# An encoder block on one NeuronCore: w_down of three groups by Strassen's seven products, alternating with the next group's w_up

## The chip, the cores and the metric

The kernel runs on one core of a Trainium2 chip. The metric is the device time in microseconds of one execution, taken as the median of the runs; lower is better. A core has five engines that run side by side, each with its own in-order instruction stream: PE (TensorE, matrix products into PSUM), DVE (VectorE) and POOL (GpSimd) for elementwise work, ACT (ScalarE) for activations and copies, and SP (SyncE), which here issues all the DMAs.

## The reference, cut to what matters

One layer over 512 tokens and 1024 channels: an RMSNorm, a wide input projection, three token mixers (a state-space layer, a pooling mixer, banded attention), a gated merge, and then the MLP that the change is in:

```
h  = h + merged @ w_out                       # 512 x 1024
hn = rmsnorm(h, norm_mlp)
h  = h + square(relu(hn @ w_up)) @ w_down     # w_up 1024 x 4096, w_down 4096 x 1024
out = rmsnorm(h, norm_final)
```

All data is float32.

## The kernel before, in words

**Three products for one.** Every float32 matrix is split into a high part (rounded to the matmul's input format, fp32r) and a low part (what is left). A product is then high x high + high x low + low x high: `mm3` (L119) issues three matmuls. ACT makes the high part by a copy and DVE the low part by a subtraction.

**Weights.** All weight pieces stand in one list, `pieces`, in the order of their use; a piece has 128 partitions x 1024 elements (512 KB). `raw_to` (L172) lets SP load piece after piece into three `raw` buffers; `split_ops` (L182) gives the two instructions that split one into `wh` and `wl`, which have two buffers each. `use(i)` (L223) is called when the product with piece i begins, and schedules the split of piece i+1.

**What sets the order.** The program is written out by hand. A counter, `tick()` (L136), advances by one after each group of three matmuls, and `later(n, f)` (L132) puts `f` into the streams of its engines n ticks on. A tick is thus a place in the program, not a wait: an engine runs ahead of PE as far as its operands and buffers allow.

**The MLP.** The 4096 hidden columns are worked in four groups of 1024 (L1311). For each group, eight *units* of w_up: one 128-column piece of w_up stands still, and the 512 tokens of `hT` move past it, so eight `mm3` over the 1024 input channels fill one PSUM tile (24 matmuls of 128x512). `relu2` (L1302) takes it out: relu on ACT (L1306), the square on DVE (L1307), the high copy on ACT, the low part on DVE. Then `tokmajor` (L394) multiplies the group with w_down, first for the output columns 0 to 511, then for 512 to 1023: four PSUM tiles of 128 tokens x 512 columns, and for each of eight 128-row slices of w_down (two in a piece) and each of the four token tiles one `mm3`. That is 96 matmuls for a half and 192 for a group. `add_all` (L1250) adds the four tiles to the residual `h_t` on DVE. In the last group the second half is done token tile by token tile (`tok_inner`, L1259), so that the final norm of a tile overlaps the next one's product; for that the pieces of its second half are of kind "z" and keep their split tiles.

**Memory.** The elementwise tiles come from one pool `z` of 38 tiles of 128x512.

Of the kernel before, what the change touches and what calls it, by code (L numbers as in the profile page):

```python
# [9 lines left out]
F32 = mybir.dt.float32  # L10
# [45 lines left out]
def trunk(ctx: ExitStack, tc: tile.TileContext, a: dict, out):  # L56
# [4 lines left out]
    def pool(name, bufs=1, **kw):  # L61
        return ctx.enter_context(tc.tile_pool(name=name, bufs=bufs, reuse_waits="tile", **kw))
# [7 lines left out]
    xT_p = pool("xT")  # L70
    raw_p = pool("raw", NRAW)
    w_p = pool("w", 2)
    z_p = pool("z", NZ)
    ps_p = pool("ps", 8, space=PSUM)

    def z(dt=F32, n=512):
# [85 lines left out]


    pieces = []
    state = {"raw": 0, "split": 0}
    raws, splits = {}, {}

    def add_piece(src, kind="w"):
        pieces.append((src, kind))
        return len(pieces) - 1  # L170

    def raw_to(i):  # L172
        while state["raw"] <= min(i, len(pieces) - 1):
            k = state["raw"]
# [5 lines left out]
            state["raw"] += 1  # L180

    def split_ops():  # L182

        i = state["split"]
        state["split"] += 1
        src, kind = pieces[i]
        A, B = src.shape[1], src.shape[2]
        box = {}
        he = VE if i == 0 else SE

        def high():
# [12 lines left out]
        def low():
            r = box["r"]
            if kind == "z":
                for k in range(A):
                    tt(box["l"][k], r[:, k], fr(box["h"][k]), SUB)
            else:
                l = w_p.tile([128, 1024], F32R, tag="wl", name="wl")[:, 0:A * B].rearrange("p (a b) -> p a b", a=A)  # L210
# [3 lines left out]
            raw_to(i + NRAW)  # L214

        return high, low

# [47 lines left out]
    P_up, P_dn = [], []  # L265
    for g in range(4):
        P_up.append([add_piece(cols(w_up, 1024 * g + 128 * m)) for m in range(8)])
        P_dn.append([[], []])
        for x in range(8):
            i, hf = (x // 2, x % 2) if g == 3 else (x % 4, x // 4)  # L270
            P_dn[g][hf].append(add_piece(rows(w_down, 8 * g + 2 * i, 2, 512 * hf), "wz"[hf] if g == 3 else "w"))
# [6 lines left out]
    kz = [[const.tile([128, 512], F32R, name=f"kz{b}{r}") for r in range(2)] for b in range(2)]  # L278
    for b in range(2):
        for r in range(2):  # L280
            GE.memset(fr(kz[b][r][64 - 64 * b:128 - 64 * b]), 0.0)

    def gvec(name):
        g = gv_p.tile([128, D], F32, tag="g", name="g")
# [15 lines left out]
    right1 = tc.alloc_tile_pool(name="s5", bufs=1, side="right", reuse_waits="tile")  # L300
    prep_p = tc.alloc_tile_pool(name="prep", bufs=1, side="right", reuse_waits="tile")
    XS = right1.tile([128, 64, 2, 2, 16], F32, name="XS")
    Ud = tc.dram_tile([512, 512], F32, name="Ud")
    Fd = tc.dram_tile([2, 8, 4, 2, 512], F32, name="Fd")
    Kd = tc.dram_tile([512, 240], F32, name="Kd")
# [993 lines left out]
        norm_rows(t, g_mlp, hn_t[t])  # L1299
    g_fin = gvec("norm_final")  # L1300

    def relu2(p, aT_h, aT_l):  # L1302
        r, h, l = z(), zr(), zr()
        aT_h.append(h)
        aT_l.append(l)
        SE.activation(out=r, in_=p, func=AF.Relu)  # L1306
        later(1, lambda: tt(r, r, r, MUL))  # L1307
        later(2, lambda: copy(SE, h, r))
        later(3, lambda: tt(l, r, fr(h), SUB))

    for g in range(4):  # L1311
        aT_h, aT_l = [], []
        m0 = 0
        if g == 0:

            us = []
            for half in range(2):
                o = slice(256 * half, 256 * half + 256)
                for m in range(2):
                    if half == 0:  # L1320
                        us.append((splits[P_up[0][0]] if m == 0 else use(P_up[0][1]), ps()))
                    (hs, ls), p = us[m]
                    for k in range(8):
                        mm3(p[:, o], hs[k], ls[k], hT_h[k][:, o], hT_l[k][:, o], k == 0, k == 7)
                        if k % 2 == 1 and half == 1:
                            tick()
                if half == 0:
                    to_feature(hn_t[3], hh_, hl_, 3)
            for m in range(2):
                relu2(us[m][1], aT_h, aT_l)  # L1330
            m0 = 2
        for m in range(m0, 8):
            run(unit_quanta(P_up[g][m], hT_h, hT_l, lambda p: relu2(p, aT_h, aT_l)))
        add_all(0, tokmajor(P_dn[g][0], aT_h, aT_l))
        if g < 3:
            add_all(1, tokmajor(P_dn[g][1], aT_h, aT_l))
    for t in range(3):
        p = tok_inner(P_dn[3][1], aT_h, aT_l, t)
# [15 lines left out]
    for q in range(2):  # L1354
        p = ps()
        c, hc = slice(256 * q, 256 * q + 256), slice(512 + 256 * q, 768 + 256 * q)
        for k in range(8):
            hs, ls = splits[P_dn[3][1][k // 2]]
# [13 lines left out]
    ts(o[:, 512:768], hg[:, 512:768], rs, 1.0, MUL, MUL)  # L1372
    SP.dma_start(out=out[tok, 512:768], in_=o[:, 512:768])
    h_p.release()

# [67 lines left out]
```

## Time and profile before

| | us |
|---|---|
| median of 3 runs | 963.36 (959.46 to 963.53) |
| the profiled execution, its own time | 961.09 |
| its span from the first to the last instruction | 959.3 |
| PE busy in the span | 935.1 (97%) |
| DVE busy | 543.1 (57%) |
| ACT busy | 404.5 (42%) |
| POOL busy | 248.9 (26%) |

The engines overlap, so the busy times don't add up to the span. The profile's line on the ended chain follows the work backwards from the last instruction, at each step to what released it, and gives each engine its share of the span. A matmul row's length includes its way through the array, and successive matmuls overlap; how fast they follow one another is read from the distance of their starts. The first w_up unit of the MLP is taken out at 613.1 us of the span, and the MLP reaches to its end.

### The profile page before, as it was taken

What the parts mean: (1) busy time and instruction counts of PE and PEld (TensorE: products, weight loads), DVE (VectorE), ACT (ScalarE), POOL (GpSimd) and SP (SyncE); (2) the same over time, 40 slices, a digit from 0 to 9 for tenths busy, and PEclk for the clock granted to TensorE, in tenths of its full rate; (3) what the DMA queues carried; (4) which work ended last, traced back from release to release, by engine and by line L of the source; (5) the groups of instructions that cost most, each with busy time, mean ns of one, the idle gap of its engine ahead of it and who ended that gap; (6) DMA issues with size and microseconds to landing.
All of it is one profiled execution on the core that took longest, in us unless ns stands there. A gap on an engine that the chain in (4) does not pass through costs nothing.

```text
span 959.3 us, 12810 instructions
## 1 busy us (share of the span) xinstructions
PE 935.1 (97%) x4755; PEld 751.1 (78%) x4755; DVE 543.1 (57%) x892; ACT 404.5 (42%) x662; POOL 248.9 (26%) x402
## 2 busy tenths in 40 slices
PE   8999899999999999998999999999999999999997
PEld 5788667777677888886878888888888888888886
DVE  4688778886644765568555355443344345334443
ACT  5634656666654334455343333432133123313432
POOL 0600355556788885243100001000000000000002
PEclk9999989999999999999999999999999999999999
DMA  9237666642222334344512373223332332323322
GB/s 312 87 111 203 169 168 179 162 133 83 83 66 75 93 101 128 98 126 122 152 45 88 110 239 90 66 88 110 91 97 97 108 89 89 110 88 90 109 88 87
DMA packets 140462, 111.05 MB, mean 116 GB/s; under 512 B 16368, under 2 KB 117104, under 8 KB 140400
## 3 DMA queue, kind: packets, MB, share of 16 engines
q1 hardware_dynamic: 140400, 110.24, 38.9%
q8 instruction: 37, 0.61, 0.3%
q14 instruction: 25, 0.20, 0.1%
HBM read 106.32 MB, written 3.90 MB: 115 GB/s over the span
## 4 chain that ended last, share of the span: by engine, by line
PE 85%; DVE 6%; DMA 3%; issue 2%; ACT 1%; SPq 1%; POOL 1%; POOLq 0%; DVEq 0%; ACTq 0%
PE ps L122 25%; PE ps L123 25%; PE ps L121 25%; PE ps L781 3%; PE ps L765 2%; DVE z L103 2%; DVE z L106 1%; DVE wl L103 1%; PE ps L735 1%; PE ps L734 1%; DMA z<-in_s_bq_im_dram 1%; DVE S L738 1%; ACT z L96 1%; DMA z<-in_xT_dram 1%; SPq L1078 1%
## 5 line engine op out<-in xcount | busy, mean ns | idle before, releaser
L103 DVE TENSOR_TENSOR wl<-raw,wh 128x1024 fp32r<-128x1024 f32 (+1 forms) x137 | 172.8, 1261 | 157.7 <-ACT wh L96 157.2
L96 ACT ACTIVATE wh<-raw 128x1024 fp32r<-128x1024 f32 (+1 forms) x136 | 142.9, 1051 | 136.3 <-PE ps L123 99.8
L121 PE MATMUL ps<-xh,wh 128*128 128x512 f32 x384 | 156.5, 407 | 0.0
L103 DVE TENSOR_TENSOR z<-z 128x512 f32<-128x512 f32 (+1 forms) x132 | 102.2, 777 | 93.1 <-ACT z L1306 60.8
L123 PE MATMUL ps<-xh,wl 128*128 128x512 f32 x384 | 150.7, 392 | 2.9 <-DVE wl L103 2.9
L122 PE MATMUL ps<-xl,wh 128*128 128x512 f32 x384 | 150.2, 391 | 0.0
L122 PE MATMUL ps<-wl,z 128*128 128x512 f32 x320 | 125.5, 392 | 3.2 <-DVE wl L103 3.2
L121 PE MATMUL ps<-wh,z 128*128 128x512 f32 x320 | 125.6, 393 | 1.8 <-ACT z L318 0.9
L123 PE MATMUL ps<-wh,z 128*128 128x512 f32 x320 | 125.5, 392 | 0.2
L109 POOL TENSOR_SCALAR sm<-sm 128x1 f32<-128x1 f32 (+1 forms) x16 | 3.6, 223 | 459.6 <-ACT hn L1285 434.0
L122 PE MATMUL ps<-hl,wh 128*128 128x512 f32 (+1 forms) x272 | 102.5, 377 | 0.3 <-DVE hl L103 0.3
L121 PE MATMUL ps<-hh,wh 128*128 128x512 f32 (+1 forms) x272 | 102.5, 377 | 0.3 <-ACT hh L96 0.3
L123 PE MATMUL ps<-hh,wl 128*128 128x512 f32 (+1 forms) x272 | 102.4, 377 | 0.0
L96 ACT ACTIVATE z<-ps 128x512 f32<-128x512 f32 (+4 forms) x128 | 72.9, 578 | 64.5 <-PE ps L123 24.2
L123 PEld LDWEIGHTS ps<-xh,wl 128*128 128x128 f32 x384 | 72.3, 188 | 19.1 <-DVE wl L103 3.3
L121 PEld LDWEIGHTS ps<-xh,wh 128*128 128x128 f32 x384 | 72.7, 189 | 14.1 <-PE ps L781 0.8
L122 PEld LDWEIGHTS ps<-xl,wh 128*128 128x128 f32 x384 | 72.7, 189 | 12.9
L109 POOL TENSOR_SCALAR S<-S,sm 128x512 f32<-128x512 f32 x64 | 59.2, 942 | 81.2 <-DMA z<-Ud 58.6
L122 PEld LDWEIGHTS ps<-wl,z 128*128 128x128 f32 x320 | 60.5, 189 | 17.0 <-DVE wl L103 4.5
L121 PEld LDWEIGHTS ps<-wh,z 128*128 128x128 f32 x320 | 60.5, 189 | 15.6 <-ACT z L318 1.9
L123 PEld LDWEIGHTS ps<-wh,z 128*128 128x128 f32 x320 | 60.4, 189 | 13.4 <-DVE z L106 1.0
L745 ACT ACTIVATE S<-S,sm 128x512 f32<-128x512 f32 x64 | 46.2, 722 | 57.6 <-DVE sm L109 52.4
(183 smaller groups left out, 1437.9 us busy)
## 6 DMA issues: line engine op xcount, KB each, us to landing
raw<-in_w_in_dram SPq DMA_DIRECT2D x55, 512.0 KB
raw<-in_w_up_dram SPq DMA_DIRECT2D x32, 512.0 KB
raw<-in_w_down_dram SPq DMA_DIRECT2D x32, 512.0 KB
T<-in_ttab_dram SPq DMA_DIRECT2D x16, 448.0 KB
z<-Fd SPq DMA_DIRECT2D x16, 256.0 KB
raw<-in_w_branch_attn_dram SPq DMA_DIRECT2D x8, 512.0 KB
raw<-in_w_out_dram SPq DMA_DIRECT2D x8, 512.0 KB
z<-in_xT_dram SPq DMA_DIRECT2D x8, 256.0 KB
```

What stands on the lines that cost most here:

```text
L96: SE.activation(out=o, in_=i, func=AF.Copy, scale=scale)
L103: (eng or VE).tensor_tensor(out=o, in0=i, in1=j, op=op)
L106: VE.scalar_tensor_tensor(out=o, in0=i, scalar=s, in1=j, op0=op0, op1=op1)
L109: (eng or VE).tensor_scalar(out=o, in0=i, scalar1=s1, scalar2=s2, op0=op0, op1=op1)
L121: TE.matmul(o, wh, xh, start=first, stop=False)
L122: TE.matmul(o, wh, xl, start=False, stop=False)
L123: TE.matmul(o, wl, xh, start=False, stop=last)
L734: TE.matmul(p, lh, khh[h], start=True, stop=False)
L735: TE.matmul(p, lh, kll[h], start=False, stop=True)
L745: SE.activation(out=s, in_=s, func=AF.Exp, bias=nm, accum_out=den[h][:, t:t + 1])
L765: TE.transpose(p[:, t * 128:t * 128 + 128], probs[h][t][:, kt * 128:kt * 128 + 128], ident)
L781: TE.matmul(p[64 * b:64 * b + 64], vt[kt][h // 8][:, c:c + 64], pts.pop((h, kt)), start=kt == 0, stop=kt == 3)
```

## The change

In groups 0, 1 and 2 the 512 x 1024 by 1024 x 1024 product with w_down is cut into halves in all three directions, and the eight products of a 256-token half with a 512 x 512 block of w_down become the seven of Strassen's method (in Winograd's form, with shared sums). The blocks of the activation are A11, A12, A21, A22 (tokens by hidden columns), and those of w_down B11 to B22.

**Sums.** S1 to S4 are sums of activation blocks (S1 and S2 on DVE, S3 and S4 on POOL), T1 to T4 sums of w_down blocks (POOL, each in two pieces). T2, T3 and T4 are written over B11, B12 and B21. Each sum is an instruction over 128x1024 elements. Splitting into high and low parts comes after the sums: a piece of kind "s" is split from a block of w_down or from a T, and `a_split` splits a block of the activation.

**Products.** `product(g, x)` is 2 pieces x 2 slices x 2 token tiles x 3 matmuls of 128x512. The results of products that share terms stay in the same PSUM tiles: the chain "b" runs through products 2, 4 and 6, "c" through 3 and 5, and after each of these two tiles are added to `h_t`. Product 0 goes to two tiles `X` in SBUF, which POOL adds to `h_t` once, after the third group.

**Order.** Product x of group g is followed by unit x of group g+1, and unit 7 of group g+1 stands alone behind product 6. `plan(g)` gives the places of the sums, splits and loads. A product is 8 ticks and a unit is 8 ticks, so a group takes 120 ticks, and product x starts at tick 16x.

**Other parts.** `use` schedules two pieces ahead where a piece of kind "s" is near; `wh` and `wl` have a third buffer during the MLP. The square of the relu moves from DVE to ACT, written in place into a tile `R` of 128 x 4 x 512; high and low parts of the activation are made later, in groups 0 to 2 by `a_split` and in the last group by `a3`. w_down of groups 0 to 2 is loaded by `b_load` into tiles of its own, not into `raw`. The last group's product with w_down is done as before, by `tokmajor` and `tok_inner`.

The core of the diff:

```diff
     def use(i):
...
         d = SPLIT_AT
+        if "s" in [kind for _, kind in pieces[i:i + 3]]:
+            j, d = i + 2, 1
...
+    DN = ("11", "21", "T2", "T1", "T3", "22", "T4")
...
+    def relu2(p, g, m):
...
+        SE.activation(out=r, in_=p, func=AF.Relu)
+        later(1, lambda: SE.activation(out=r, in_=r, func=AF.Square))
...
+    AN = ("A11", "A12", "S2", "S1", "S3", "S4", "A22")
+
+    def a_split(g, x):
...
+    def b_load(g, nm):
+        k0, c0 = (0, 4)[nm[0] == "2"], (0, 512)[nm[1] == "2"]
+        for q in range(2):
+            t = Bt[g, nm, q] = str_p.tile([128, 2, 512], F32, tag=f"B{nm}{q}", name=f"B{nm}")
+            SP.dma_start(out=t, in_=rows(w_down, 8 * g + k0 + 2 * q, 2, c0))
+
+    def b_sum(g, nm, q, i, j, op):
+
+        at = {"T2": "11", "T3": "12", "T4": "21"}.get(nm)
+        o = Bt[g, at, q] if at else str_p.tile([128, 2, 512], F32, tag=f"{nm}{q}", name=nm)
+        tt(o, Bt[g, i, q], Bt[g, j, q], op, GE)
+        Bt[g, nm, q] = o
...
+    def plan(g):
...
+        at(4, *a_split(g, 1))
+        at(6, lambda: a_sum(g, "S1", lambda: ra[:, :, T1], lambda: rb[:, :, T1], ADD, VE))
+        at(8, lambda: a_sum(g, "S2", S("S1"), lambda: ra[:, :, T0], SUB, VE))
+        at(18, *a_split(g, 2))
+        at(22, lambda: a_sum(g, "S4", lambda: rb[:, :, T0], S("S2"), SUB, GE))
+        for n, x in ((34, 3), (50, 4), (66, 5), (82, 6)):
+            at(n, *a_split(g, x))
+        for q in range(2):
+            at(2 + 4 * q, lambda q=q: b_sum(g, "T3", q, "22", "12", SUB))
+            at(12 + 4 * q, lambda q=q: b_sum(g, "T2", q, "T3", "11", ADD))
+            at(36 + 4 * q, lambda q=q: b_sum(g, "T4", q, "21", "T2", SUB))
+        if g < 2:
+            for n, nm in ((44, "11"), (76, "12"), (92, "22"), (108, "21")):
+                at(n, lambda nm=nm: b_load(g + 1, nm))
+            at(112, lambda: b_t1(g + 1))
...
+    CH = (("a", None), ("d", (0, 0)), ("b", (0, 1)), ("c", (1, 1)), ("b", (1, 1)), ("c", (0, 1)), ("b", (1, 0)))
+
+    def product(g, x):
...
+                    TE.matmul(acc[t], ah[:, k, o], hs[i], start=st, stop=False, **kw)
+                    TE.matmul(acc[t], al[:, k, o], hs[i], start=False, stop=False, **kw)
+                    TE.matmul(acc[t], ah[:, k, o], ls[i], start=False, stop=sp, **kw)
+                    tick()
+        for t in range(2):
+            if to is None:
+                later(1 + t, lambda t=t: add_x1(g, t, acc[t]))
+            else:
+                later(1 + t, lambda t=t: add_to(2 * to[0] + t, to[1], acc[t]))
...
-    for g in range(4):
-        aT_h, aT_l = [], []
...
-        for m in range(m0, 8):
-            run(unit_quanta(P_up[g][m], hT_h, hT_l, lambda p: relu2(p, aT_h, aT_l)))
-        add_all(0, tokmajor(P_dn[g][0], aT_h, aT_l))
-        if g < 3:
-            add_all(1, tokmajor(P_dn[g][1], aT_h, aT_l))
...
+    def a3(m):
+        h, l = zr(), zr()
         aT_h.append(h)
         aT_l.append(l)
...
+        r = R[3, m // 4][:, m % 4]
+        copy(SE, h, r)
+        tt(l, r, fr(h), SUB)
...
+    for g in range(3):
+        plan(g)
+        for x in range(7):
+            product(g, x)
+            up_unit(g + 1, x)
+        if g == 2:
...
+            for m in range(4):
+                later(2 * m, lambda m=m: a3(m))
+        up_unit(g + 1, 7)
+    for m in range(4, 8):
+        later(2 * m - 7, lambda m=m: a3(m))
+    for n in range(8):
+        later(2 + 2 * n, lambda n=n: x1_out(n // 2, n % 2))
+    add_all(0, tokmajor(P_dn3[0], aT_h, aT_l))
```

On PE, before, the last three matmuls of group 0's last unit (`hh`, `hl` are the tokens, `wh`, `wl` the split weights) and the first three with w_down (`z` is the activation's high, then low part):

```order
L121 MATMUL ps<-hh,wh 128x512
L122 MATMUL ps<-hl,wh 128x512
L123 MATMUL ps<-hh,wl 128x512
L121 MATMUL ps<-wh,z 128x512
L122 MATMUL ps<-wl,z 128x512
L123 MATMUL ps<-wh,z 128x512
```

Behind these follow 189 more of the same form.

On PE, now, the end of group 0's first product (`ah`, `al` are the split block of the activation) and the beginning of group 1's first unit:

```order
L1443 MATMUL ps<-wh,ah 128x512
L1444 MATMUL ps<-wh,al 128x512
L1445 MATMUL ps<-wl,ah 128x512
L121 MATMUL ps<-hh,wh 128x512
L122 MATMUL ps<-hl,wh 128x512
L123 MATMUL ps<-hh,wl 128x512
```

Of the matmuls the form stays, and their order moved: runs of 192 with w_down and 192 with w_up become runs of 24 of either. PE's whole stream has 3835 rows before and 3763 now.

The second place is in the last group, where `tokmajor` begins behind the last w_up unit. On ACT, before: the high part of the first w_down piece, then the last unit's relu (L1306) and high part, a "z" piece, and the high part of the second w_down piece:

```order
L96 ACTIVATE wh<-raw 128x1024
L1306 ACTIVATE z<-ps 128x512
L96 ACTIVATE z<-z 128x512
L96 ACTIVATE z<-raw 128x512 x2
L96 ACTIVATE wh<-raw 128x1024
```

Between the relu and the second piece's `wh` stand three copies.

On ACT, now, at the same place, from the last unit's relu on (L1344 relu, L1345 square, `z<-R` the high parts of `a3`):

```order
L1344 ACTIVATE R<-ps 128x512
L1345 ACTIVATE R<-R 128x512
L96 ACTIVATE z<-R 128x512
L96 ACTIVATE z<-raw 128x512 x2
L96 ACTIVATE z<-R 128x512 x2
L96 ACTIVATE wh<-raw 128x1024
```

Between them stand now a square and five copies.

On DVE at the same place, before (the first piece's `wl`, the square and the low part of the last unit, the two low parts of a "z" piece, the second piece's `wl`, the next "z" piece):

```order
L103 TENSOR_TENSOR wl<-raw,wh 128x1024
L103 TENSOR_TENSOR z<-z 128x512 x2
L103 TENSOR_TENSOR z<-raw,z 128x512 x2
L103 TENSOR_TENSOR wl<-raw,wh 128x1024
L103 TENSOR_TENSOR z<-raw,z 128x512 x2
```

Behind the last unit's square, three low parts stand ahead of the second piece's.

On DVE there, now, from the low parts of `a3` for hidden slices 0 and 1 on:

```order
L103 TENSOR_TENSOR z<-R,z 128x512 x2
L103 TENSOR_TENSOR wl<-raw,wh 128x1024
L103 TENSOR_TENSOR z<-R,z 128x512 x4
L103 TENSOR_TENSOR z<-raw,z 128x512 x2
L103 TENSOR_TENSOR z<-R,z 128x512
L103 TENSOR_TENSOR wl<-raw,wh 128x1024
```

Of the four `z<-R,z` in a row, those of slices 2 and 3 belong to the unit before; behind the last relu stand slices 4, 5 and 6, ahead of the second piece's `wl`.

## Rows read from the trace of the kernel before

**Rows 1.** The page: busy time by engine, and shares of the ended chain.
```profile
PE 935.1 (97%) x4755; PEld 751.1 (78%) x4755; DVE 543.1 (57%) x892; ACT 404.5 (42%) x662; POOL 248.9 (26%) x402
...
PE 85%; DVE 6%; DMA 3%; issue 2%; ACT 1%; SPq 1%; POOL 1%; POOLq 0%; DVEq 0%; ACTq 0%
```

**Rows 2.** Busy time by stretch (us, instructions), granted clock, DMA share; about one group.
```profile
core 0: us, PE busy (x) PEld busy (x) DVE busy (x) ACT busy (x) POOL busy (x), PEclk, DMA share, GB/s
...
690.00:780.00 90.00, 90.00 (x399) 74.55 (x398) 37.86 (x43) 26.98 (x33) 0.00 (x0) 1.00 0.32 99
```

**Rows 3.** What PE waited for from 600 to 960 us, in total (us, times, longest).
```profile
PE ps L122 <- DVE hl L103: 0.3, 1, 0.3
PE ps L121 <- ACT hh L96: 0.3, 1, 0.3
```

**Rows 4.** Timeline of PE where the last group's w_down begins (start, length).
```profile
908.70 0.39 PE L121 MATMUL ps<-wh,z 128*128 128x512 f32 x1
...
914.14 0.39 PE L121 MATMUL ps<-wh,z 128*128 128x512 f32 x1
914.36 0.39 PE L122 MATMUL ps<-wl,z 128*128 128x512 f32 x1
```

**Rows 5.** Timeline of ACT at the same place (in brackets the idle time before).
```profile
903.46 0.60 ACT L1306 ACTIVATE z<-ps 128x512 f32<-128x512 f32 x1 [2.50 <-PE ps L123]
...
908.90 0.60 ACT L1306 ACTIVATE z<-ps 128x512 f32<-128x512 f32 x1 [2.50 <-PE ps L123]
910.25 0.63 ACT L96 ACTIVATE z<-z 128x512 fp32r<-128x512 f32 x1 [0.76 <-DVE z L103]
910.79 1.14 ACT L96 ACTIVATE z<-raw 128x512 fp32r<-128x512 f32 x2
911.83 1.04 ACT L96 ACTIVATE wh<-raw 128x1024 fp32r<-128x1024 f32 x1
...
916.19 1.06 ACT L96 ACTIVATE wh<-raw 128x1024 fp32r<-128x1024 f32 x1 [2.28 <-DMA raw<-in_w_down_dram]
```

**Rows 6.** Timeline of DVE at the same place.
```profile
911.53 1.29 DVE L103 TENSOR_TENSOR z<-raw,z 128x512 fp32r<-128x512 f32 x2
912.91 1.23 DVE L103 TENSOR_TENSOR wl<-raw,wh 128x1024 fp32r<-128x1024 f32 x1
```

**Rows 7.** DVE's groups by form, 600 to 950 us (busy us, mean ns).
```profile
L103 DVE TENSOR_TENSOR wl<-raw,wh 128x1024 fp32r<-128x1024 f32 x58 | 71.1, 1225 | 88.6 <-ACT wh L96 88.5
L103 DVE TENSOR_TENSOR z<-z 128x512 fp32r<-128x512 f32 x32 | 22.1, 692 | 21.1 <-ACT z L96 21.0
...
L103 DVE TENSOR_TENSOR h<-ps,h 128x512 f32<-128x512 f32 x32 | 21.9, 690 | 19.2 <-PE ps L123 19.2
```

**Rows 8.** ACT's groups by form, 600 to 950 us; L1275 is a square.
```profile
L96 ACT ACTIVATE wh<-raw 128x1024 fp32r<-128x1024 f32 x58 | 61.0, 1052 | 105.2 <-PE ps L123 91.8 <-issue 7.7 <-PE ps L122 3.2
L96 ACT ACTIVATE z<-z 128x512 fp32r<-128x512 f32 x32 | 20.2, 633 | 23.0 <-DVE z L103 23.0
L1306 ACT ACTIVATE z<-ps 128x512 f32<-128x512 f32 x32 | 19.1, 598 | 82.2 <-PE ps L123 82.2
...
L1275 ACT ACTIVATE hn<-h 128x512 f32<-128x512 f32 x4 | 2.5, 632 | 15.8 <-DVE h L103 15.8
```

**Rows 9.** POOL's sums of 128x512 in the attention stage: ns min/median/max, first and last start.
```profile
L103 POOL TENSOR_TENSOR z<-z x24: 1262/1677/2260, 116.2 to 480.7; 128x512 f32<-128x512 f32 x24
L103 POOL TENSOR_TENSOR z<-z,PT x16: 1102/1550/2089, 367.8 to 439.1; 128x512 f32<-128x512 f32 x16
```

**Rows 10.** Timelines of POOL and DVE where both do sums, around 412 us.
```profile
411.31 3.38 POOL L103 TENSOR_TENSOR z<-z 128x512 f32<-128x512 f32 x2 [3.48 <-DVE z L106]
414.65 4.68 POOL L103 TENSOR_TENSOR z<-z,PT 128x512 f32<-128x512 f32 x3
...
413.47 2.31 DVE L103 TENSOR_TENSOR wl<-raw,wh 128x1024 fp32r<-128x1024 f32 x1
416.77 1.59 DVE L103 TENSOR_TENSOR z<-z 128x512 f32<-128x512 f32 x1 [0.99 <-POOL z L103]
```

**Rows 11.** What SP's DMA queue waited for, 600 to 960 us (us, times, longest).
```profile
SPq L178 <- DVE wl L103: 279.9, 57, 7.9
```

More of the change, by code (lines that the diff above doesn't have):

```diff
@@ L169, in add_piece, with raw_to @@
         pieces.append((src, kind))
+        if kind != "s":
+            loaded.append(len(pieces) - 1)
         return len(pieces) - 1
[L172 to L174 removed]
+    def raw_to(n):
+        while state["raw"] <= min(n, len(loaded) - 1):
+            k = loaded[state["raw"]]
             src = pieces[k][0]
@@ L264, in trunk, with add_up @@
             P_wo[hf].append(add_piece(rows(w_out, 2 * i, 2, 512 * hf), "wz"[hf]))
-    P_up, P_dn = [], []
-    for g in range(4):
[L267 to L271, printed above, removed]
+    DN = ("11", "21", "T2", "T1", "T3", "22", "T4")
+    Bt = {}
+    P_up = [[] for _ in range(4)]
+    P_st, P_dn3 = [], [[], []]
+    def add_up(g, m):
+        P_up[g].append(add_piece(cols(w_up, 1024 * g + 128 * m)))
+    for m in range(8):
+        add_up(0, m)
+    for g in range(3):
+        P_st.append([])
+        for x, nm in enumerate(DN):
+            P_st[g].append([add_piece(lambda g=g, nm=nm, q=q: Bt[g, nm, q], "s") for q in range(2)])
+            add_up(g + 1, x)
+        add_up(g + 1, 7)
+    for x in range(8):
+        i, hf = x // 2, x % 2
+        P_dn3[hf].append(add_piece(rows(w_down, 24 + 2 * i, 2, 512 * hf), "wz"[hf]))
     ident = const.tile([128, 128], F32, name="ident")
@@ L302, in trunk @@
     XS = right1.tile([128, 64, 2, 2, 16], F32, name="XS")
+    kz = [[right1.tile([128, 512], F32R, name=f"kz{b}{r}") for r in range(2)] for b in range(2)]
+    for b in range(2):
+        for r in range(2):
+            GE.memset(fr(kz[b][r][64 - 64 * b:128 - 64 * b]), 0.0)
     Ud = tc.dram_tile([512, 512], F32, name="Ud")
@@ new lines, in add_to, with add_x1 @@
+    def add_to(t, hf, p):
+        o = h_t[t][:, 512 * hf:512 * hf + 512]
+        tt(o, p, o, ADD)
+    def add_x1(g, t, p):
+        if g == 0:
+            copy(SE, X1[t], p)
+        else:
+            tt(X1[t], p, X1[t], ADD)
+    chain = {}
+    CH = (("a", None), ("d", (0, 0)), ("b", (0, 1)), ("c", (1, 1)), ("b", (1, 1)), ("c", (0, 1)), ("b", (1, 0)))
+    def product(g, x):
+        nm, to = CH[x]
+        first = (g, nm) not in chain
+        if first:
+            chain[g, nm] = [ps(), ps()]
+        acc = chain[g, nm]
+        for q in range(2):
+            hs, ls = use(P_st[g][x][q])
+            ah, al = A_hl[g, x]
+            for i in range(2):
+                k = 2 * q + i
+                for t in range(2):
+                    o = slice(128 * t, 128 * t + 128)
+                    st, sp = first and k == 0, k == 3
+                    kw = {} if first else {"skip_group_check": True}
+                    TE.matmul(acc[t], ah[:, k, o], hs[i], start=st, stop=False, **kw)
+                    TE.matmul(acc[t], al[:, k, o], hs[i], start=False, stop=False, **kw)
+                    TE.matmul(acc[t], ah[:, k, o], ls[i], start=False, stop=sp, **kw)
+                    tick()
+        for t in range(2):
+            if to is None:
+                later(1 + t, lambda t=t: add_x1(g, t, acc[t]))
+            else:
+                later(1 + t, lambda t=t: add_to(2 * to[0] + t, to[1], acc[t]))
@@ new lines, in trunk @@
+    us = []
+    for half in range(2):
+        o = slice(256 * half, 256 * half + 256)
+        for m in range(2):
+            if half == 0:
+                us.append((splits[P_up[0][0]] if m == 0 else use(P_up[0][1]), ps()))
+            (hs, ls), p = us[m]
+            for k in range(8):
+                mm3(p[:, o], hs[k], ls[k], hT_h[k][:, o], hT_l[k][:, o], k == 0, k == 7)
+                if k % 2 == 1 and half == 1:
+                    tick()
+        if half == 0:
+            to_feature(hn_t[3], hh_, hl_, 3)
@@ L1304, in relu2 @@
+    for m in range(2):
+        relu2(us[m][1], 0, m)
+    for n, nm in ((4, "11"), (8, "12"), (16, "22"), (24, "21")):
+        later(n, lambda nm=nm: b_load(0, nm))
+    later(40, lambda: b_t1(0))
+    later(30, lambda: a_sum(0, "S3", lambda: R[0, 0][:, :, T0], lambda: R[0, 0][:, :, T1], SUB, GE))
+    for n, f in enumerate(a_split(0, 0)):
+        later(36 + n, f)
+    for m in range(2, 8):
+        up_unit(0, m)
+    aT_h, aT_l = [], []
+    def a3(m):
+        h, l = zr(), zr()
         aT_h.append(h)
```

99 lines of the change are left out of this document (61 added, 38 removed).

## The prediction

> **What bounds the kernel now.** I read the page's busy times first: PE is busy 97% of the span and holds 85% of the ended chain, DVE and ACT hold little [rows 1]. Then the table by stretch, because an average could hide a stage with another limit. In a stretch of about one MLP group PE is busy for all of 90.00 us at the full granted clock, DVE for 37.86, ACT for 26.98 and POOL not at all [rows 2]. From 600 us to the end PE waited twice, 0.3 us each [rows 3]. So in the stage that is changed only PE's work counts: a matmul less shortens the span by one matmul, as long as DVE, ACT and POOL keep bringing operands in time. The busy length of 0.39 us must not be used for it, since matmuls overlap. Two relus that follow successive units of 24 matmuls lie 908.90 - 903.46 = 5.44 us apart [rows 5], which is 0.2267 us a matmul; the first w_down piece of the last group agrees, 24 matmuls from 908.70 to 914.14 [rows 4]. A tick (three matmuls) is 0.68 us.
>
> **What is removed on PE.** A group with w_down was 192 matmuls, and is now 7 x 2 x 2 x 2 x 3 = 168. Three groups save 3 x 24 = 72, the 72 rows by which PE's stream is shorter. Their form is unchanged, 128x128 against 128x512, and from w_up to w_down PE went on before without a gap [rows 3, 4], so I cost the alternation itself at nothing. 72 x 0.2267 = 16.3 us off the path. This is the ceiling of the gain.
>
> **What is added beside PE.** A Strassen group, with the next group's units, lasts (168 + 192) x 0.2267 = 81.6 us on PE.
> - DVE had 8 squares, 8 low parts of 128x512, 16 of 128x1024 and 8 adds. It has now 14 + 8 low parts of w pieces, 7 of activation blocks, S1 and S2, and 14 adds: 31 x 1.225 + 14 x 0.69 = 47.6 us [rows 7].
> - ACT: 8 relus at 0.598, 8 squares at 0.63 (the nearest row is a square over 512 elements) and 29 copies at 1.052: 40.3 us [rows 8]; in group 0 two copies of X more, 1.2 us.
> - POOL: ten sums of 128x1024 a group. No row shows that size. From below, twice the shortest sum of 128x512, 2 x 1.10 = 2.2 us; from above, twice the longest, 2 x 2.26 = 4.5 us, with the waits for DVE in it [rows 9]. I take 2.2 to 3.3 (twice the medians), 22 to 33 us a group.
> - SP loads as many bytes as before.
> Each is far under 81.6, so none is a bound by its volume. What is left is lateness, place by place.
>
> **Lateness in the Strassen groups.** The tightest step is the split of the w_up piece, which begins with product x and is due in the unit behind it. From the product's start: relu at +0.20 as now [rows 4, 5], square at +0.85, high part at +1.39 (a copy of 512 elements is followed after 0.54 us, 910.25 to 910.79 [rows 5]) to +2.43, low part to +3.7. PE needs the low part with the unit's third matmul, at 5.44 + 0.45 = +5.89: 2.2 us to spare. The two "s" pieces are scheduled two pieces ahead, and have 5 us and more; the third buffer of `wh` and `wl` frees them one tick before they are scheduled. T2 is the longest chain: T3 and T2 are four sums, and the second piece of T2 can begin when B11 is split, some 6 ticks ahead of the group; with 3.3 us it is there at tick 0, and its split stands at tick 25. Loads of w_down can stand behind one of w_up that waits for DVE, on average 279.9 / 57 = 4.9 us and at most 7.9 [rows 11]; the last of them before a group that is in a hurry, B21 at tick 108, is due at tick 125, 11.6 us later. The transfer itself took 3.3 us in the last group: a buffer came free at 911.53 + 1.29 = 912.82 [rows 6], and ACT had the data at 916.19 [rows 5]. That leaves little when the longest wait comes first, and enough otherwise.
>
> The new thing is that POOL sums run beside DVE's. Rows show what that does: a low part of 1.225 us took 2.31 while POOL did sums, and one of 0.69 took 1.59 [rows 7, 10]. The loss, 1.1 and 0.9 us, is about a whole POOL sum of 128x512 (shortest 1.10). So a DVE instruction can be held by one sum, here of 2.2 us, which just uses up the 2.2 us to spare. From below the cost is zero (POOL can't shorten anything, and the sums have no other price on PE); from above, with 3.3 us a hold, 1.1 us late at a unit, and with POOL busy 33 of 81.6 us that is 24 x 0.40 x 1.1 = 10.6 us. I take 0.5 us, near the lower end, since the hold that the rows show scales to 2.2.
> The Trainium skill, SBUF — State Buffer, section "Who interferes with whom", says that a DVE instruction with two SBUF inputs contends with a GpSimd instruction that reads SBUF, and that the loser is blocked for the whole instruction; the trace agrees (2.31 against 1.225 us [rows 7, 10]). Had they shared bandwidth instead, every DVE sum would be a little slower, none would be held for 2.2 us, and this term would be zero; by the rule the rival of the held splits, below, is open.
>
> **Lateness where the last group's w_down begins.** Before, this place is just in time: the low part of the second piece ends at 912.91 + 1.23 = 914.14 [rows 6], and PE's first use of it is at 914.36 [rows 4]. Now more stands ahead of it in the same queues. On ACT, by the same clock: relu 908.90, square 909.55, five copies at about 0.53 from 910.09, then the second piece's high part from 912.74 to 913.78. On DVE: the low part of slice 4 from 910.76, that of slice 5 when its high part is done, 912.3 to 913.0, the "z" piece's two to 914.2, slice 6 to 914.9, and only then the second piece's, to 916.1. PE is 1.7 us late, once. The third piece is due 5.44 us later, at 919.8, with the lateness 921.5; its buffer comes free with the "z" piece at 914.2, its load takes 3.3 us and its split 1.05 + 1.23, so it is there at 919.8. The lateness is then neither made up nor repeated. POOL's additions of X don't fall in here: they wait for the last adds to `h_t` at tick 106 at the latest, and eight of them at 1.7 us, half of which can go earlier, end before `tokmajor`. From below this term is zero (if ACT takes the copies sooner), from above 1.7 + 1.1 = 2.8 us (if one of the sums ahead is held by POOL after all [rows 10]).
>
> **The sum.** The profiled execution's own time is 961.1 us (its span 959.3 and 1.8 around it), 2.3 under the median of the three runs, which spread over 4 us. 961.1 - 16.3 + 0.5 + 1.7 = 947.0 us.
>
> **Rivals.**
> - *No lateness at all*: 961.1 - 16.3 = 944.8. For it: PE waits for nothing now [rows 3]. Against it: the spare 0.2 us at the last group's beginning [rows 4, 6].
> - *Held splits*: POOL's sums make the w_up splits late by up to 1.1 us at the units they meet, 10.6 us in all, 961.1 - 16.3 + 10.6 + 1.7 = 957.1. For it: the held low parts [rows 10]. Against it: most places have 5 us to spare, and POOL's sums come in bunches.
> - *Slower: DVE becomes the bound.* If each POOL sum holds DVE for h us, DVE needs 47.6 + 10 h in a group, and exceeds PE's 81.6 from h = 3.4; the whole gain is gone when each group is (16.3 - 1.7) / 3 = 4.9 us longer, 47.6 + 10 h = 81.6 + 4.9, h = 3.9. With h = 4.5, the upper bound [rows 9], it is 11 us a group: 961.1 - 16.3 + 33 + 1.7 = 980. For it: the bound isn't excluded. Against it: the longest sums contain their own waits for DVE, so they can't be taken as a hold.
> - *The change doesn't do what it says*: excluded for the count of matmuls, by PE's stream.
>
> **How the numbers follow.** The forecast has 0.73, no lateness 0.10, held splits 0.12, slower 0.05. The forecast's own range is 945 to 950 (the bounds of the last group's term, the first two us of the holds, and the run-to-run spread). The range for 8 in 10 is 943 to 954: below by the spread of the runs under 944.8, above by half of the held splits. What can be told from no change is 0.5%, 4.8 us, so faster is under 956.3. Of the held splits about half reach over that, and of the slower rival a fifth stays within 0.5%: faster 0.73 + 0.10 + 0.06 = 0.89, same 0.06 + 0.01 = 0.07, slower 0.04.
>
> **What would show it.** Right: 72 matmuls fewer at starts 0.227 us apart; in the three groups PE's idle time under 2 us and its waits for `wl`; one wait of 1 to 3 us for DVE at the second w_down piece of the last group; POOL busy 22 to 33 us a group; some low parts lengthened from 1.2 to 3.4 us. Wrong: PE waiting at most of the units, ACT stopped by a POOL sum or a load of w_down (a T or B tile that comes late), matmuls farther apart in the alternation, or POOL sums over 3.4 us with DVE busy throughout.

## The result, and the profile after

The changed kernel takes 947.43 us, the median of 4 runs (945.39 to 947.93). The kernel before took 962.2 us in runs beside it (959.46 to 963.53). The ratio is 0.984, with a 95% interval of 0.9822 to 0.9859. The forecast was 947.0 us, in a range from 943 to 954. The profiled execution took 945.39 us, with a span of 943.5 us (959.3 before).

The page of the changed kernel, busy time by engine and shares of the ended chain, as in [rows 1]:

```profile
PE 920.4 (98%) x4683; PEld 739.0 (78%) x4683; DVE 589.6 (62%) x897; ACT 446.3 (47%) x711; POOL 342.7 (36%) x440
...
PE 87%; DVE 6%; ACT 2%; issue 2%; DMA 2%; POOL 1%; SPq 0%; POOLq 0%; DVEq 0%; ACTq 0%
```

PE has 72 rows less (4755 to 4683) and is busy 14.7 us less. The other three are busy 41.8 to 93.8 us more, and their shares of the chain hardly moved (DVE and POOL not at all, ACT from 1 to 2%).

The same 90 us of the span as in [rows 2], busy time of PE, PEld, DVE, ACT and POOL, granted clock, DMA share and GB/s:

```profile
690.00:780.00 90.00, 90.00 (x398) 74.52 (x398) 60.25 (x51) 42.97 (x51) 29.66 (x11) 1.00 0.32 102
```

PE is still busy for all of it at the upper of the clock's two levels (2.4 GHz). DVE went from 37.86 to 60.25, ACT from 26.98 to 42.97, POOL from nothing to 29.66.

What PE waited for from 600 us to the end (us in total, times, longest), as in [rows 3]:

```profile
PE ps L122 <- DVE wl L103: 1.4, 1, 1.4
PE ps L122 <- DVE hl L103: 0.3, 1, 0.3
PE ps L121 <- ACT hh L96: 0.2, 1, 0.2
```

One wait is new. PE's timeline shows where it is, at the second w_down piece of the last group, as in [rows 4]:

```profile
890.80 0.39 PE L121 MATMUL ps<-wh,z 128*128 128x512 f32 x1
...
896.24 0.39 PE L121 MATMUL ps<-wh,z 128*128 128x512 f32 x1
898.07 0.50 PE L122 MATMUL ps<-wl,z 128*128 128x512 f32 x1 [1.44 <-DVE wl L103]
```

The first piece runs at the old cadence, 24 matmuls from 890.80 to 896.24. The next matmul was due at 896.47 and started at 898.07: 1.6 us late. The view lists only 1.44, since a row of 0.39 us covers the first 0.16 us behind the 0.227 of the spacing. A lateness below 0.16 us therefore never shows as idle time in this view. The matmul behind the late one starts 0.33 us after it, 0.10 more than the spacing, so the wait costs 1.7 us in all.

**Where the time went.** The same events cut both spans into three parts: the second and the last relu of the MLP's 32. The units' rows on ACT, first in the kernel before:

```profile
615.11 0.60 ACT L1306 ACTIVATE z<-ps 128x512 f32<-128x512 f32 x1 [1.45 <-PE ps L123]
```

and in the changed kernel:

```profile
613.38 0.60 ACT L1344 ACTIVATE R<-ps 128x512 f32<-128x512 f32 x1 [2.28 <-PE ps L123]
...
891.00 0.60 ACT L1344 ACTIVATE R<-ps 128x512 f32<-128x512 f32 x1 [1.15 <-PE ps L123]
891.63 0.63 ACT L1345 ACTIVATE R<-R 128x512 f32<-128x512 f32 x1
892.17 0.62 ACT L96 ACTIVATE z<-R 128x512 fp32r<-128x512 f32 x1
892.69 1.14 ACT L96 ACTIVATE z<-raw 128x512 fp32r<-128x512 f32 x2
893.73 1.14 ACT L96 ACTIVATE z<-R 128x512 fp32r<-128x512 f32 x2
894.77 1.05 ACT L96 ACTIVATE wh<-raw 128x1024 fp32r<-128x1024 f32 x1
```

The last relu of before is at 908.90 [rows 5].

| stretch | before | after | difference |
|---|---|---|---|
| start to the MLP's second relu | 615.11 | 613.38 | -1.7 |
| second to last relu (the MLP stretch below) | 293.79 | 277.62 | -16.2 |
| last relu to the end | 50.4 | 52.5 | +2.1 |
| span | 959.3 | 943.5 | -15.8 |

The first part has the same work in both kernels. In the changed kernel and its variants below it ends between 612.87 and 619.01 us, so -1.7 is taken as variation from run to run and not as a gain. The second part is the change. The third is the change only in part: PE's last matmul shows how much.

```profile
952.43 0.28 PE L123 MATMUL ps<-z 128*128 128x256 f32 x1
```

before, and in the changed kernel:

```profile
936.24 0.28 PE L123 MATMUL ps<-z 128*128 128x256 f32 x1
```

From the first matmul of the last group's w_down (908.70 and 890.80) to this one it is 43.73 us before and 45.44 after, 1.71 more, which is the wait. The other 0.4 us lies behind the last matmul, where 6.87 us were left before and 7.26 after; in the kernels below with the same wait this rest is 6.80 to 7.31, so the 0.4 is taken as variation too.

### The profile page after: what moved, and what is told of

Read it like the earlier page. It is cut to its first block, busy times and chain, and to the rows that moved or that the text cites. A ratio compares the mean times of both kernels' runs of the same rounds, so it can differ in the third digit from the quotient of the medians.

```text
span 943.5 us, 12801 instructions
## 1 busy us (share of the span) xinstructions
PE 920.4 (98%) x4683; PEld 739.0 (78%) x4683; DVE 589.6 (62%) x897; ACT 446.3 (47%) x711; POOL 342.7 (36%) x440
## 4 chain that ended last, share of the span: by engine, by line
PE 87%; DVE 6%; ACT 2%; issue 2%; DMA 2%; POOL 1%; SPq 0%; POOLq 0%; DVEq 0%; ACTq 0%
PE ps L122 22%; PE ps L121 22%; PE ps L123 22%; PE ps L1444 4%; PE ps L1445 4%; PE ps L1443 4%; PE ps L810 3%; PE ps L794 2%; DVE z L103 1%; ACT z L96 1%; PE ps L1124 1%; PE ps L764 1%; PE ps L763 1%; DVE S L767 1%; DVE wl L103 1%
## 5 line engine op out<-in xcount | busy, mean ns | idle before, releaser
L103 DVE TENSOR_TENSOR wl<-raw,wh 128x1024 fp32r<-128x1024 f32 (+1 forms) x113 | 159.6, 1414 | 169.8 <-ACT wh L96 169.0
L123 PE MATMUL ps<-xh,wl 128*128 128x512 f32 x384 | 150.7, 393 | 2.9 <-DVE wl L103 2.9
L96 ACT ACTIVATE wh<-raw 128x1024 fp32r<-128x1024 f32 (+1 forms) x112 | 117.5, 1049 | 35.3 <-PE ps L123 7.9
L123 PE MATMUL ps<-hh,wl 128*128 128x512 f32 (+1 forms) x272 | 102.5, 377 | 0.0
L123 PEld LDWEIGHTS ps<-xh,wl 128*128 128x128 f32 x384 | 72.3, 188 | 19.1 <-DVE wl L103 3.3
L1344 ACT ACTIVATE R<-ps 128x512 f32<-128x512 f32 x32 | 19.1, 598 | 128.2 <-PE ps L123 128.2
L103 POOL TENSOR_TENSOR z<-z 128x512 f32<-128x512 f32 x24 | 39.4, 1661 | 92.8 <-DVE z L106 42.2
L1443 PE MATMUL ps<-wh,ah 128*128 128x512 f32 x168 | 65.4, 389 | 0.0
L1444 PE MATMUL ps<-wh,al 128*128 128x512 f32 x168 | 65.4, 389 | 0.0
L1445 PE MATMUL ps<-wl,ah 128*128 128x512 f32 x168 | 65.4, 389 | 0.0
L103 DVE TENSOR_TENSOR z<-z 128x512 f32<-128x512 f32 (+1 forms) x68 | 55.7, 824 | 10.5 <-ACT z L96 7.0
L103 POOL TENSOR_TENSOR B<-B,B 128x1024 f32<-128x1024 f32 x18 | 51.3, 2865 | 28.8 <-DVE wl L103 14.0
```

The costliest lines, as they stand in the source:

```text
L96: SE.activation(out=o, in_=i, func=AF.Copy, scale=scale)
L103: (eng or VE).tensor_tensor(out=o, in0=i, in1=j, op=op)
L123: TE.matmul(o, wl, xh, start=False, stop=last)
L1443: TE.matmul(acc[t], ah[:, k, o], hs[i], start=st, stop=False, **kw)
L1444: TE.matmul(acc[t], al[:, k, o], hs[i], start=False, stop=False, **kw)
L1445: TE.matmul(acc[t], ah[:, k, o], ls[i], start=False, stop=sp, **kw)
```

## The experiments

The table has all runs. "MLP" is the stretch from the second to the last relu, "end" the one from there to the span's end, both in the profiled execution.

| kernel | median us (range) | ratio to before (95%) | MLP | end |
|---|---|---|---|---|
| changed kernel | 947.43 (945.39 to 947.93) | 0.984 (0.9822 to 0.9859) | 277.6 | 52.5 |
| the same, run again | 948.67 (945.60 to 949.78) | 0.986 (0.9839 to 0.9882) | 277.8 | 52.5 |
| last group's split later | 946.97 (945.81 to 948.52) | 0.9849 (0.9829 to 0.9870) | 277.5 | 50.8 |
| the same, run again | 946.50 (945.66 to 949.45) | 0.9848 (0.9826 to 0.9869) | 277.9 | 50.8 |
| an eighth product | 964.54 (961.28 to 967.89) | 1.0023 (1.0001 to 1.0044) | 294.0 | 52.6 |
| no sums on POOL | 947.48 (945.63 to 948.47) | 0.9852 (0.9833 to 0.9870) | 277.5 | 52.1 |
| the sums on DVE | 947.40 (945.66 to 948.56) | 0.9854 (0.9831 to 0.9877) | 277.5 | 52.1 |
| 21 sums on POOL | 975.48 (973.53 to 977.32) | 1.0142 (1.0122 to 1.0162) | 304.1 | 52.1 |
| two weight buffers | 957.37 (956.41 to 957.62) | 0.9952 (0.9937 to 0.9967) | 286.2 | 52.3 |
| two weight buffers, no sums | 948.71 (947.01 to 950.63) | 0.9866 (0.9845 to 0.9886) | 277.5 | 52.3 |
| blocks, not alternating | 967.82 (964.48 to 969.72) | 1.0069 (1.0051 to 1.0087) | 296.5 | 52.5 |
| blocks, no sums | 950.59 (949.31 to 951.50) | 0.9884 (0.9865 to 0.9903) | 279.4 | 52.1 |

### Are the 72 matmuls the whole gain? An eighth product

Product 6 is issued twice, the second time into PSUM tiles that nobody reads, so that a group has its 192 matmuls with w_down again and all else stays:

```diff
+        dead = [ps(), ps()] if x == 6 else None
...
+                    if dead:
+                        mm3(dead[t], ah[:, k, o], al[:, k, o], hs[i], ls[i], k == 0, k == 3)
```

> In each of the three groups product 6 is issued twice, the second time into PSUM tiles that nothing reads: 24 matmuls more a group, 72 in all, with no other instruction added. The result is unchanged. Theory (the whole gain is PE's 72 matmuls at 0.2267 us; the alternation and the third weight buffer give nothing by themselves): 947.4 + 16.3 = 963.7 us, the kernel before plus the one wait of the last group. Rival (part of the gain comes from the new order, the third buffer or earlier splits): under 960 us. Rival (the alternation costs something that hides under the gain): over 966 us.

The MLP stretch is 294.0 us against 277.6: 16.4 us come back for 72 matmuls, 0.227 each, and it stands at the 293.8 of the kernel before. PE's waits are those of the changed kernel. So the seven products give all of the gain; the alternation, the third weight buffer and the move of the square are worth nothing on PE by themselves as long as operands come in time.

### The 1.6 us at the last group: its splits later

The low parts of the last four activation slices are scheduled six ticks later, behind the second w_down piece:

```diff
-        later(2 * m - 7, lambda m=m: a3(m))
+        later(2 * m - 1, lambda m=m: a3(m))
```

> The high and low parts of hidden slices 4 to 7 of the last group are placed at ticks 7, 9, 11 and 13 of the last group's first half instead of 1, 3, 5 and 7, so that they stand behind the split of the second w_down piece. Theory (PE's one wait in the changed kernel comes from the operations queued ahead of that split): the wait of 1.4 us in the trace, 1.6 us at the starts, is gone, no other takes its place, and the time is 947.4 - 1.6 = 945.8 us. Rival (DVE or ACT lacks the time there at all): the wait moves to the third piece or to slice 4, and the time stays at 947.4.

The wait for `wl` is gone from PE's list, which holds nothing over 0.3 us, and PE's part from the first matmul with w_down to the last is 43.71 us, as before the change. DVE's row of the second piece's low part in this kernel:

```profile
899.15 1.23 DVE L103 TENSOR_TENSOR wl<-raw,wh 128x1024 fp32r<-128x1024 f32 x1 [0.18 <-ACT wh L96]
```

and PE's first use of it, on time at 0.227 behind the matmul before:

```profile
901.10 0.39 PE L121 MATMUL ps<-wh,z 128*128 128x512 f32 x1
901.33 0.39 PE L122 MATMUL ps<-wl,z 128*128 128x512 f32 x1
```

The low part now ends at 900.38, 0.95 us ahead. The end part is 50.8 us instead of 52.5.

The median didn't tell the two kernels apart, so both ran again side by side.

> The changed kernel once more, as it is, to have its time on the same chip and in the same call as the next one: 947.4 us, within 1 us.

> The kernel with the high and low parts of slices 4 to 7 later, once more, beside the changed kernel on the same chip. Theory: 1.6 us less than that, 945.8 us. Rival: no difference, since the wait is only seen in the profiled execution.

The changed kernel, run again, took 948.67 us, 1.3 above what was expected of it. The later split was 2.2 us faster here and 0.5 us the first time, with overlapping intervals; by the ratio to the kernel before it wasn't faster the first time (0.9849 against 0.984). The traces show 52.5 and 50.8 us for the end part, twice each, and 45.44 and 45.46 against 43.71 and 43.71 us for PE's part of it. The 1.7 us are shown in the traces, and the times alone don't resolve them. The version has the lowest medians, 946.97 and 946.50 us, by less than the runs of one kernel differ.

### Do POOL's sums cost PE anything? No sums, and the sums on DVE

In the first kernel POOL's ten sums of a group are left out and one operand stands for each:

```diff
+        if eng is GE:
+            S_t[g, nm] = i()
+            return
...
+        at = {"T2": "11", "T3": "12", "T4": "21", "T1": "12"}[nm]
+        Bt[g, nm, q] = Bt[g, at, q]
```

> The ten sums of a group on POOL are left out (S3, S4 and T1 to T4 are replaced by one of their operands, so the result of the three groups is not the product); all splits, products and loads stay. Theory (POOL's sums hold DVE instructions, but each hold ends inside the spare time before PE): PE's work and waits stay, 947.4 us, within 1 us; the longest low parts fall from 3.4 to 1.2 us. Rival (held splits cost PE time that the waits don't show): 2 to 10 us less, 937 to 945 us.

In the second, all ten are on DVE (`GE` becomes `VE` in `b_sum` and in the calls for S3 and S4).

> The ten sums of a group run on DVE instead of POOL, at the same places in the program. DVE's own work in a group rises by 10 x 1.22 = 12.2 us to about 60 of 81.6 us, and nothing holds it any more (31 instructions a group that POOL's sums, 2.4 us each, could hold). Theory (DVE has the room, PE the only bound): 947.4 us, within 1.5 us. Rival (a sum that waits for a load of w_down or for a split now stops all of DVE, in order): PE waits at several places in a group and the time rises by 5 us or more.

Both are at the time of the changed kernel, 947.48 and 947.40 us. The MLP stretch is 277.47 us in both, which is 1224 matmuls of 0.2267; the changed kernel was at 277.62 and 277.84, and the one with later splits at 277.47 and 277.86. What the sums on POOL cost is thus 0 to 0.4 us. The sums do hold DVE. The longest low parts of the changed kernel, by tile (ns min/median/max, first and last start):

```profile
L103 DVE TENSOR_TENSOR al<-S,ah x12: 1211/1219/3419, 661.1 to 856.3; 128x1024 fp32r<-128x1024 f32 x12
```

and the same of those that are left without the sums:

```profile
L103 DVE TENSOR_TENSOR al<-S,ah x6: 1219/1220/1220, 662.7 to 836.8; 128x1024 fp32r<-128x1024 f32 x6
```

A hold is there, 2.2 us, and the spare time of its place swallows it. With the sums on DVE, DVE was busy 60.94 us of the same 90, against 60.25 with the holds and 48.60 with neither: to it the holds weigh about as much as the sums themselves.

### Where is the point at which DVE binds? 21 sums

S3 is computed four times, S4 three times, T1 twice, and an addition to T4 is made and taken back: 21 sums a group on POOL in place of ten.

```diff
+        for _ in range({"S3": 4, "S4": 3}.get(nm, 1)):
+            tt(o, i(), j(), op, eng)
...
+        if nm == "T1":
+            tt(o, Bt[g, i, q], Bt[g, j, q], op, GE)
+        if nm == "T4":
+            tt(o, o, Bt[g, j, q], ADD, GE)
+            tt(o, o, Bt[g, j, q], SUB, GE)
```

> POOL repeats sums without changing their results but for rounding: S3 four times, S4 three times, T1 twice, T4 three times (it adds T2 back and takes it off again), 21 sums a group in place of 10, 2.4 us each without waits. DVE's splits and activation sums with two operands in SBUF take 31 x 1.22 = 37.8 us of a group, its adds from PSUM 9.5 us. Theory (a POOL sum and such a DVE instruction exclude each other for their whole length, so that from some point DVE is the bound): the two together need 37.8 + 21 x 2.4 = 88 us at least and 98 with the adds, against PE's 81.6; the time rises by 15 to 45 us, to 962 to 992 us, PE waiting for DVE's low parts at many units. Rival (they share, or the exclusion costs only where it meets a tight place): under 953 us.

The MLP stretch is 26.5 us longer. What PE waited for in this kernel (the two lines that are new; L1451 is the third matmul of a product's `mm3`, whose line number moves with the edits):

```profile
PE ps L1451 <- DVE wl L103: 13.2, 19, 4.2
PE ps L123 <- DVE wl L103: 2.9, 9, 0.3
```

In its worst 40 us DVE has no gap while PE does (busy of PE, PEld, DVE, ACT, POOL, granted clock):

```profile
650.00:690.00 40.00, 34.27 (x137) 26.52 (x138) 40.00 (x17) 15.92 (x19) 37.33 (x12) 0.96 0.15 42
```

DVE's timeline there:

```profile
672.57 3.42 DVE L103 TENSOR_TENSOR al<-S,ah 128x1024 fp32r<-128x1024 f32 x1
675.91 3.41 DVE L103 TENSOR_TENSOR wl<-B,wh 128x1024 fp32r<-128x1024 f32 x1
679.25 1.27 DVE L103 TENSOR_TENSOR h<-ps,h 128x512 f32<-128x512 f32 x2
680.44 2.23 DVE L103 TENSOR_TENSOR wl<-B,wh 128x1024 fp32r<-128x1024 f32 x1
```

and POOL's, five sums in one row, 3.35 us each:

```profile
678.20 16.77 POOL L103 TENSOR_TENSOR B<-B,B 128x1024 f32<-128x1024 f32 x5
```

The two engines take turns: each instruction with two SBUF operands waits for one of the other's. The two adds with an operand in PSUM run at their own length (1.27 us for two) beside POOL's sum. The slower rival's mechanism is real. It is not there at ten sums and is there at 21; where between them it begins was not run.

### What the third weight buffer is for: two buffers, with and without sums

The line that gives `wh` and `wl` a third buffer during the MLP is taken away:

```diff
-    state["wide"] = mlp_p
```

> The third buffer of wh and wl is taken away; nothing else changes. A split of the w_up piece and of the second piece of a product can then begin only 4 ticks before it is due, 2.72 us, and takes 0.2 + 1.04 + 1.22 = 2.5 us. Theory (spare time is what keeps POOL's holds off PE): without a hold it is just in time (0.45 us more until the low part's matmul), with a hold of up to 2.4 us it is up to 1.7 us late; 42 such places, POOL busy about 40% of the time: 8 to 20 us more, 955 to 967 us, PE's waits being for wl. Rival (the spare time doesn't matter, holds seldom meet a split): under 950 us.

8.6 us more in the MLP stretch. PE's new waits (L1444 is here a product's third matmul, L123 a unit's):

```profile
PE ps L1444 <- DVE wl L103: 3.3, 3, 1.2
PE ps L123 <- DVE wl L103: 1.9, 6, 0.3
```

They list 5.2 us of the 8.6. At the starts each listed place costs 0.16 us more, and another 0.11 at the next matmul: with nine places that is 7.6 us, and three more units are late by 0.19 in this way, too little to be listed. These twelve places make 8.2 of the 8.6 us, and the granted clock is 1.00 throughout the MLP stretch, so the clock has no part in it. At the longest wait DVE's row and PE's are these:

```profile
718.83 3.39 DVE L103 TENSOR_TENSOR wl<-B,wh 128x1024 fp32r<-128x1024 f32 x1 [2.86 <-ACT wh L96]
722.28 0.50 PE L1444 MATMUL ps<-wl,ah 128*128 128x512 f32 x1 [1.23 <-DVE wl L103]
```

A POOL sum had started at 718.75, 0.08 us ahead of the low part, which ended at 722.22. Not held, at 1.22 us, it would have ended at 720.05, ahead of the 720.90 at which its matmul was due. The pair kernel has two buffers and no sums on POOL (the edit of the kernel without sums).

> Two buffers of wh and wl, and POOL's sums left out (one operand stands for each, so the three groups' result is not the product). With the sums, two buffers took 957.4 us, 8.6 us more from the MLP's first transposes to its last relu. Theory (that time is POOL's holds meeting splits without spare time): it comes back, 947 to 950 us, and PE waits only at the last group's second piece. Rival (two buffers are late by themselves): 955 us or more, with PE's waits for wl as before.

277.47 us again: without the sums two buffers are enough. The 8.6 us were POOL's holds, which met splits with too little spare time.

### What the alternation is for: blocks, with and without sums

The seven products of a group run in a row and then the eight units; the pieces' order, and the ticks of splits and sums, are moved with them (three of the edited lines):

```diff
     for g in range(3):
         plan(g)
         for x in range(7):
             product(g, x)
+        for x in range(7):
             up_unit(g + 1, x)
...
-        for n, x in ((34, 3), (50, 4), (66, 5), (82, 6)):
+        for n, x in ((14, 3), (22, 4), (30, 5), (38, 6)):
...
-            at(12 + 4 * q, lambda q=q: b_sum(g, "T2", q, "T3", "11", ADD))
+            at(4 + q, lambda q=q: b_sum(g, "T2", q, "T3", "11", ADD))
```

> No alternation: the seven products of a group follow one another, then the eight units of the next group; sums and splits are moved forward so that each stands ahead of its use, the instructions are the same. DVE's work for a product (two low parts of weights, one of the activation, two adds: 5.0 us) then falls into 5.44 us of PE, without S1, S2 and POOL's holds of four to five sums, while the units need 1.2 us in 5.44. Theory (the alternation is what spreads DVE's work): DVE is late by (35 + 2.4 + 5 x 2.4) - 38 = about 11 us a group, 20 to 33 us in all, 967 to 980 us, PE waiting for DVE in the products. Rival (the queues run far enough ahead, alternation isn't needed): under 953 us.

18.9 us more, and slower than the kernel before (1.0069, 1.0051 to 1.0087). PE's new waits:

```profile
PE ps L1445 <- DVE wl L103: 8.8, 5, 2.8
...
PE ps L123 <- DVE wl L103: 1.3, 2, 0.7
```

DVE at the longest of them:

```profile
654.52 3.35 DVE L103 TENSOR_TENSOR al<-S,ah 128x1024 fp32r<-128x1024 f32 x1
657.80 6.68 DVE L103 TENSOR_TENSOR wl<-B,wh 128x1024 fp32r<-128x1024 f32 x2
```

PE there, and behind it:

```profile
657.93 0.50 PE L1444 MATMUL ps<-wh,al 128*128 128x512 f32 x1
661.23 0.75 PE L1445 MATMUL ps<-wl,ah 128*128 128x512 f32 x1 [2.80 <-DVE wl L103]
661.78 0.63 PE L1443 MATMUL ps<-wh,ah 128*128 128x512 f32 x1
662.20 0.63 PE L1444 MATMUL ps<-wh,al 128*128 128x512 f32 x1
```

and the windows around it, the last but two columns the granted clock:

```profile
656.00:660.00 4.00, 2.32 (x10) 1.34 (x8) 4.00 (x2) 3.24 (x4) 4.00 (x2) 1.00 0.00 0
660.00:664.00 4.00, 2.77 (x7) 2.20 (x8) 4.00 (x2) 0.00 (x0) 3.39 (x2) 0.66 0.38 131
664.00:668.00 4.00, 4.00 (x18) 3.25 (x17) 4.00 (x6) 2.09 (x3) 0.00 (x0) 0.91 0.39 133
```

Three low parts in a row are held, PE waits, and behind the wait the clock is granted at its lower level (1.2 GHz) for a while: 0.66 over 4 us, matmuls 0.43 apart in place of 0.227. All three groups have such a place (the granted clock is 0.83 over 655 to 665, 745 to 755 and 835 to 845 us), and in the first two the matmuls behind the wait lose about 1.7 us each time. The listed 10.1 us are thus not the whole price. The pair kernel has the blocks and no sums.

> Products and units not alternated, and POOL's sums left out (the result is not the product). With the sums that order took 967.8 us, and its trace shows three DVE instructions in a row at 3.3 us in the first product, PE waiting 2.8 us, and a granted clock of 0.66 behind it. Theory A (the holds are the cause, DVE's own 37 us in 38 us of products just fits): 947 to 953 us. Theory B (DVE's own work in the products is too much): 957 to 968 us, with PE waiting for DVE though no low part is longer than 1.3 us.

279.4 us, 1.8 above the changed kernel, with none of these waits listed. So about 17 of the 18.9 us are the holds and the clock behind them, and not DVE's volume in a run of products. The 1.8 us that are left are DVE's own work: five times a product's third matmul is late, too little for the list, as here:

```profile
656.30 0.39 PE L1445 MATMUL ps<-wh,al 128*128 128x512 f32 x1
656.78 0.50 PE L1446 MATMUL ps<-wl,ah 128*128 128x512 f32 x1
```

The starts are 0.48 apart in place of 0.227, and the next 0.34. The low part, not held (1.22 us long), ended at 656.73, behind S1 in DVE's queue. Theory B's mechanism is thus there, at a tenth of its size.

## Why the prediction was right, point by point

- **What bounds the kernel**: confirmed. PE is busy for 90.00 of 90.00 us after as before, and the time follows the number of matmuls, in both directions (the eighth product).
- **72 matmuls, 16.3 us**: measured 16.2 in the MLP stretch, and 16.4 back with the eighth product.
- **The work beside PE**: in 90 us DVE is busy 60.25, which is 54.6 in a group of 81.6; the sum said 47.6, and left the holds out (without the sums, and so without their holds, it is 48.60 of the 90, or 44.1). ACT comes to 39.0 (40.3 predicted), POOL to 26.9 (22 to 33). POOL's sum, which no row of before showed, takes 2.40 us alone:

```profile
L103 POOL TENSOR_TENSOR S<-R x3: 2400/2402/2402, 625.6 to 772.5; 128x1024 f32<-128x1024 f32 x3
L103 POOL TENSOR_TENSOR B<-B,B x18: 2391/2634/3407, 633.7 to 823.3; 128x1024 f32<-128x1024 f32 x18
```

  That is near the lower bound of 2.2. No sum came near the upper one, 4.5; that this one contained POOL's own waits for DVE, as the prediction argued against the slower rival, fits, since here a sum that meets DVE's low parts takes up to 3.4.
- **Held splits, 0.5 us (0 to 10.6)**: the hold is as long as was expected, 2.2 us, and costs 0 to 0.4. The reason given was right: places with 2.2 us to spare and more. The pairs with two buffers and with blocks show it from the other side: with less to spare, the same sums cost 8.6 and 17 us. Of the two held rows that the prediction read from before, the one of 1.59 us is a sum of the attention stage and not a low part; the other, 2.31 us, carries the reading by itself. The rival of held splits at the units was false, because the third buffer and the alternation leave that spare time.
- **Lateness at the last group, 1.7 us (0 to 2.8)**: 1.6 measured at the starts, 1.7 in PE's part of the end. DVE's rows, with the queue as the prediction had it:

```profile
892.82 0.69 DVE L103 TENSOR_TENSOR z<-R,z 128x512 fp32r<-128x512 f32 x1 [1.54 <-ACT z L96]
894.38 0.69 DVE L103 TENSOR_TENSOR z<-R,z 128x512 fp32r<-128x512 f32 x1 [0.87 <-ACT z L96]
894.99 1.28 DVE L103 TENSOR_TENSOR z<-raw,z 128x512 fp32r<-128x512 f32 x2
896.19 0.68 DVE L103 TENSOR_TENSOR z<-R,z 128x512 fp32r<-128x512 f32 x1
896.79 1.22 DVE L103 TENSOR_TENSOR wl<-raw,wh 128x1024 fp32r<-128x1024 f32 x1
```

  `wl` is ready at 898.01, 7.2 us behind the first matmul of the group with w_down at 890.80; the prediction had 7.4. It is neither made up nor repeated: PE's part of the end is 1.7 us longer than before, and as before where the splits stand later.
- **The rival with no lateness** (944.8) is what the version with later splits does in its trace: an end part of 50.8, within 0.4 us of before, and 43.71 against 43.73 us on PE. **Slower** would have needed a hold of 3.9 us at ten sums; it is 2.2, and 21 sums got there. **The change doesn't do what it says** was excluded, and rightly.
- **The total**: the terms came out close one by one, but that the sum came within 0.4 us is in part luck. It starts from one execution of the kernel before (961.1; the median of its runs is 962.2), and the changed kernel's own two medians lie 1.2 us apart. In the trace the two stretches that changed add up to -16.2 + 1.7 = -14.5 us, the prediction's terms to -14.1.

The Trainium skill, SBUF — State Buffer, section "Who interferes with whom", has a DVE instruction with two SBUF inputs and a GpSimd instruction that reads SBUF contend, the loser blocked for a whole instruction. The traces agree: low parts of 1.22 us take up to 3.42 beside sums of 2.40, and the adds with an operand in PSUM are not held (no `h<-ps,h` of the changed kernel is longer than 0.69).

## What to carry to other kernels

Where PE has no gap, count matmuls and multiply by the distance of their starts; that term came out at 16.2 of 16.3 us. What is added on other engines is priced by the spare time of each place and not by volume: the same ten POOL sums a group cost 0 to 0.4 us, 8.6 us or 17 us depending on whether a third buffer and the order of the work had left 2.2 us ahead of each split. Look at the end of a regular stage, where the next stage's splits queue behind the last one's: that was the only wait added, and six ticks in one line removed it.

## What the runs showed of the hardware

- After a listed PE wait of 2.80 us (3.3 between starts), with shorter gaps around it, the granted clock of the next 4 us was 0.66, in 664 to 668 us 0.91. The listed wait is then less than its price.
- DVE's and ACT's rows overlap as PE's do: a low part of 128x1024 is 1.22 us long, two in a row take 2.35, and ACT's copies of 128x512 follow at 0.52 to 0.54 though a row is 0.62. The prediction's 47.6 us, made of whole rows, are too high by this (44.1 without holds), and too low by the holds.
- The time ahead of the MLP's second relu, with the same work, ended between 612.87 and 619.01 us, a spread that is more than most edits here moved. Distances inside one trace resolved what medians could not.
